# Layer 0's row passes: partial sums put into the PSUM banks by ScalarE, and a bias table built with one Sign pass

## The chip, the core and the metric

The kernel runs on one core of a Trainium2 chip. The metric is the device time in microseconds, the median of several runs. TensorE multiplies matrices into eight PSUM banks, VectorE, ScalarE and GpSimd do elementwise work, and SyncE's queue (SP) issues nearly all transfers. Each engine takes its instructions in order and meets the others through semaphores.

## What is computed

Two blocks on x of shape (1, 256, 2048), float32. The first has two layers:

```python
for l in range(DEPTH):                                   # two layers
    h = rmsnorm(x, norm_gain[l]) * (1 + scale) + shift   # scale, shift, gate = silu(c) @ w_mod[l] + b_mod[l]
    proj = h @ w_in[l]                                   # q_a, k_a, v_a, g_a, q_i, k_i, w_i, q_b, k_b, v_b, g_b
    # sparse attention: top 64 keys by the index scores, logits get a bias:
    bias = rel_bias[t5_bucket(pos_q - pos_k)]            # 32 buckets x 8 heads
    # retention on q_b, k_b, v_b
    x = x + gate * (concat([y_a, y_b]) @ w_out[l])
```

`t5_bucket` gives a distance of 0 to 15 its own bucket and puts larger ones into 16 buckets that widen logarithmically. The second block (convolution, a gated linear recurrence, two output projections, a gated embedding) is not touched.

## The kernel before

Float32 products are made of three matmuls each: an operand is split into a high and a low part (`hi`, `lo`), and hi x hi, hi x lo and lo x hi are summed. `wchunk` does this for weights: one transfer of two k-tiles by up to 512 columns into `raw` (512 KB, three buffers, L231), a cast on ScalarE that gives `whi` (L236), and a subtraction on VectorE that gives `wlo` (L238). `wgroup` runs over the chunks of a column group and, for each chunk, over the two row tiles t = 0, 1, with six matmuls for each (L254 to L256, in the order hi x hi, hi x lo, lo x hi); both row tiles have a bank of their own out of four (`mmt`), so two groups fit at once. When a group is done its consumer empties the two banks.

In `layer`, ten column groups of 512 (one of 336) columns are not computed at once. In layer 0 the normalized rows hT become ready in four quarters of four k-tiles, since each quarter needs a vector-matrix product with w_mod (`gemv`, 16 transfers of 512 KB and 16 VectorE multiply-adds at L357 per quarter). So the ten groups are swept four times (q = 0 to 3), two chunks a group. The consumer in these passes is `spill`: in pass q = 0 ScalarE copies each bank to a tile `held` (L931; the tiles are named sp and gate), in passes 1 to 3 VectorE adds the bank to it (L934), and pass 3 hands the sum on. Layer 1 has two passes.

From pass q = 1 on a background generator builds the bias table, advanced by 0.75 steps for each chunk (`step`, `RATE["t5"]`). `rel_rotary` writes the clipped distances as bytes to DRAM (`reld`, L422). `bias_table` reads them back spread over 128 partitions (`load`, L461, tile `rb`): partition p compares with bucket p % 32. Three ScalarE passes over 512 columns (Abs L483, Relu L484, Relu L486) make a one-hot matrix, two matmuls (L469) with the high and low part of the bias values look the biases up, ScalarE copies the result out (L471), and it is stored to DRAM (`biasd`, L472). There are 12 loads of 1024 bytes per partition; one is issued half a job ahead. `until("select")` in pass q = 3 emits what is left of it.

The order on each engine is made by a list scheduler from the order of emission and from priorities: `tc.high_priority(offset=n)` moves an instruction n places forward (`AHEAD`: 20 for a weight's transfer, 30 for its cast, 35 for its subtraction). On the chip each queue keeps the order that the scheduler gave it.

## Time and profile before

| | |
|---|---|
| median of 3 runs | 1931.42 us (1928.2 to 1932.54) |
| the profiled execution | 1935.11 us, span 1933.3 us |
| TensorE busy (matmuls) | 1841.2 us, 95% |
| VectorE busy | 1310.0 us, 68% |
| ScalarE busy | 1041.2 us, 54% |
| moved by DMA | 440.37 MB, mean 228 GB/s |

The span runs from the first to the last instruction of one execution. Busy time of TensorE is that of its matmuls, whose shown ends overlap the next matmul's start. A wait is told as the one who waited, the one who ended the wait, and the idle time before it.

### The profile page before, as it was taken

The page shows a single profiled execution, that of the slowest core. Times are in us where ns is not written, and L with a number is a line of the kernel's source. Part 1 is how long each engine was busy: PE and PEld are TensorE (multiplying, and loading weights), DVE is VectorE, ACT ScalarE, POOL GpSimd, SP SyncE. Part 2 cuts the span into 40 slices and gives each one's busy share as a digit, 9 for nine tenths or more (in the row PEclk, how much of TensorE's full clock was granted, in tenths as well). Part 3 has the DMA queues.
Part 4 walks back from the last instruction along what each step waited for, and adds up shares of the span by engine and source line. Part 5 has one row for each costly group of instructions (what it writes and reads, how often), then busy time and mean ns, then how long its engine had stood idle before and what let it go on. Part 6 is the DMA issues. An engine that isn't in the chain of part 4 may idle for free.

```text
span 1933.3 us, 24130 instructions
## 1 busy us (share of the span) xinstructions
PE 1841.2 (95%) x8670; PEld 1500.1 (78%) x8670; DVE 1310.0 (68%) x1705; ACT 1041.2 (54%) x1576; POOL 109.0 (6%) x220
## 2 busy tenths in 40 slices
PE   3989999998989999999999999999999999999997
PEld 3867677777867787788778778878887888888886
DVE  6788889988667779966655656656665545555564
ACT  3567674645445546356455764466545444445554
POOL 2000040002010005000110000000000000000100
PEclk9999999999989999999999999999999999999998
DMA  9988888887888999865557665556556666656664
GB/s 315 319 289 290 274 296 259 289 290 237 295 281 269 314 301 312 274 202 157 161 184 219 205 186 163 155 161 197 164 151 191 194 191 193 195 185 218 186 202 146
DMA packets 230921, 440.37 MB, mean 228 GB/s; under 512 B 19728, under 2 KB 32144, under 8 KB 230672
## 3 DMA queue, kind: packets, MB, share of 16 engines
q1 hardware_dynamic: 228880, 436.38, 71.3%
q10 hardware_dynamic: 1440, 2.34, 0.4%
q8 instruction: 68, 1.11, 0.2%
q14 instruction: 53, 0.43, 0.1%
q0 software_dynamic: 480, 0.10, 0.0%
HBM read 430.85 MB, written 7.91 MB: 227 GB/s over the span
## 4 chain that ended last, share of the span: by engine, by line
PE 64%; DMA 14%; DVE 10%; ACT 5%; issue 5%; POOL 2%; SPq 1%; ACTq 0%; DVEq 0%; POOLq 0%
PE mm L255 19%; PE mm L256 19%; PE mm L254 19%; DMA graw<-in_w_mod_dram 6%; DVE wlo L238 4%; DVE acc L357 2%; DMA rb<-reld 2%; DMA raw<-in_w_in_dram 2%; ACT whi L236 2%; PE tr L201 2%; DMA raw<-in_w_out_dram 1%; PE tr L1153 1%; DMA dec<-in_k_dec_dram 1%; DMA L<-biasd 1%; DMA raw<-in_w_mod_dram 1%
## 5 line engine op out<-in xcount | busy, mean ns | idle before, releaser
L238 DVE TENSOR_TENSOR wlo<-raw,whi 128x1024 fp32r<-128x1024 f32 (+1 forms) x596 | 721.0, 1212 | 408.8 <-ACT whi L236 407.0
L236 ACT CAST whi<-raw 128x1024 fp32r<-128x1024 f32 (+1 forms) x596 | 620.9, 1044 | 676.0 <-PE mm L256 437.2
L255 PE MATMUL mm<-wlo,ah 128*128 128x512 f32 (+1 forms) x2368 | 933.6, 394 | 14.1 <-DVE wlo L238 13.8
L254 PE MATMUL mm<-whi,ah 128*128 128x512 f32 (+1 forms) x2368 | 933.8, 397 | 13.7 <-ACT ah L192 7.8
L256 PE MATMUL mm<-whi,al 128*128 128x512 f32 (+1 forms) x2368 | 931.0, 393 | 0.5 <-DVE al L193 0.3
L255 PEld LDWEIGHTS mm<-wlo,ah 128*128 128x128 f32 x2368 | 447.5, 189 | 119.8 <-DVE wlo L238 32.6
L254 PEld LDWEIGHTS mm<-whi,ah 128*128 128x128 f32 x2368 | 446.4, 189 | 109.7 <-ACT whi L236 10.4
L256 PEld LDWEIGHTS mm<-whi,al 128*128 128x128 f32 x2368 | 447.1, 189 | 93.0 <-DVE al L193 2.4
L357 DVE SCALAR_TENSOR_TENSOR acc<-graw,ct,acc 128x1024 f32<-128x1024 f32 x174 | 222.7, 1280 | 51.5 <-DMA graw<-in_w_mod_dram 50.9
L934 DVE TENSOR_TENSOR sp<-sp,mm 128x512 f32<-128x512 f32 (+1 forms) x64 | 41.8, 657 | 8.4 <-PE mm L256 8.2
L201 PE MATMUL tr<-blob,ev 128*128 128x128 f32 x192 | 35.8, 277 | 11.5 <-DVE ev L1181 3.8
L184 ACT ACTIVATE ev<-tr,vT 128x128 f32<-128x128 f32 x112 | 32.4, 375 | 17.1 <-PE tr L201 17.1
L201 PEld LDWEIGHTS tr<-blob,ev 128*128 128x128 f32 x192 | 24.1, 141 | 21.2 <-issue 8.4
L156 POOL TENSOR_SCALAR rv<-tot 128x1 f32<-128x1 f32 (+1 forms) x9 | 2.8, 307 | 660.2 <-DVE tot L208 646.8
L504 ACT ACTIVATE junk<-xs 128x512 bf16<-128x512 f32 (+1 forms) x42 | 25.6, 610 | 22.1 <-DMA xs<-in_x_dram 10.0
L158 POOL TENSOR_TENSOR ry<-rv,mhalf 128x4 f32<-128x4 f32 (+2 forms) x33 | 31.8, 965 | 2.7
L201 PE MATMUL tr<-blob,xs 128*128 128x128 f32 x128 | 24.2, 281 | 5.3 <-ACT xs L995 3.6
L1153 PEld LDWEIGHTS tr<-X 128*128 128x128 f32 x224 | 27.0, 192 | 2.0 <-ACT uT L1203 1.0
L483 ACT ACTIVATE oh<-rb,blob 128x512 f32<-128x512 uint8 x24 | 16.4, 717 | 22.5 <-DMA rb<-reld 22.5
L1153 PE MATMUL tr<-X 128*128 128x128 f32 x224 | 27.5, 276 | 0.1
L156 POOL TENSOR_SCALAR rv<-ssq 128x4 f32<-128x4 f32 x12 | 4.5, 371 | 402.4 <-ACT junk L504 402.2
L156 POOL TENSOR_SCALAR rv<-var 128x4 f32<-128x4 f32 x8 | 5.2, 645 | 361.5 <-DVE var L853 361.3
(275 smaller groups left out, 1227.3 us busy)
## 6 DMA issues: line engine op xcount, KB each, us to landing
raw<-in_w_in_dram SPq DMA_DIRECT2D x416, 512.0 KB
graw<-in_w_mod_dram SPq DMA_DIRECT2D x186, 512.0 KB
raw<-in_w_out_dram SPq DMA_DIRECT2D x64, 512.0 KB
raw<-in_w_o_dram SPq DMA_DIRECT2D x32, 512.0 KB
raw<-in_w_ple_gate_dram SPq DMA_DIRECT2D x32, 512.0 KB
raw<-in_w_a_out_dram SPq DMA_DIRECT2D x16, 512.0 KB
raw<-in_w_b_out_dram SPq DMA_DIRECT2D x16, 512.0 KB
raw<-in_w_in_dram SPq DMA_DIRECT2D x16, 256.0 KB
```

Of the source, the lines that this page charges most:

```text
L158: G.tensor_tensor(y, v, mhalf[:, 0:n], op=OP.pow)
L184: A.activation(e[:, s], ps[:, s], AF.Copy, scale=gain[:, i:i + 1])
L201: T.transpose(ps[:, s], src[:, s], ident)
L236: A.copy(hi, raw)
L238: V.tensor_sub(lo, raw, hi.bitcast(F32))
L254: T.matmul(o, ah, hi[:, j, :], start=first, stop=False)
L255: T.matmul(o, ah, lo[:, j, :], start=False, stop=False)
L256: T.matmul(o, al, hi[:, j, :], start=False, stop=end)
L357: last[0] = V.scalar_tensor_tensor(acc, rf, ct[:, j:j + 1], acc, op0=OP.mult, op1=OP.add)
L504: A.activation(junk[:, :n], src, AF.Square, accum_out=acc)
L934: V.tensor_add(h, h, pt[:, :n])
L1153: T.matmul(ps[:, h * P:(h + 1) * P], X[:, h, s], X[:, h, s], start=True, stop=True)
```

## The change

In passes 1 and 2 of layer 0 VectorE no longer adds the bank to `held`. Instead ScalarE copies `held` into the bank before the group's first matmul, which then accumulates on it (`start` is false), and copies the bank out again at the group's end, as in pass 0. The copies in get a priority offset of 10. Pass 3 and layer 1 stay.

The one-hot matrix becomes a matrix of signs of (distance + 0.5 - lower edge), one ScalarE pass of 512 columns; the bias values are replaced by half differences between neighbouring buckets (`rsh` holds the values shifted by one bucket), so that the signed sum gives the same bias. There are 6 loads of 2048 bytes per partition, two are issued at the start, and the load for job n + 2 is issued with the last pass of job n, into the buffer which that pass reads. Six empty steps stand between the first loads and the first pass.

```diff
+            if sums:
+                with tc.high_priority(offset=AHEAD["sums"]):      # 10
+                    for t in (0, 1):
+                        A.copy(pts[t][:, :n], sums[t][:, :n])
@@ mms
-                    first = ci == 0 and j == 0
+                    first = ci == 0 and j == 0 and not sums
@@ bias_table
+            rsh = ap.tile([P, 32], F32, name="rsh", tag="dec", bufs=2)
+            V.memset(rsh, 0.0)
             for g in range(4):
-                G.dma_start(rbd[32 * g:32 * g + 32, 8 * g:8 * g + 8], a["rel_bias"])
+                c = slice(8 * g, 8 * g + 8)
+                G.dma_start(rbd[32 * g:32 * g + 32, c], a["rel_bias"])
+                G.dma_start(rsh[32 * g + 1:32 * g + 32, c], a["rel_bias"][0:31])
+                G.dma_start(rsh[32 * g:32 * g + 1, c], a["rel_bias"][31:32])
+            V.scalar_tensor_tensor(rbd, rsh, turn, rbd, op0=OP.mult, op1=OP.add)
+            V.tensor_scalar(rbd, rbd, 0.5, None, op0=OP.mult)
@@
-            jobs = [(0, r) for r in range(0, 32, 8)] + [(1, r) for r in range(0, 32, 4)]
+            jobs = [(0, 0), (0, 16)] + [(1, r) for r in range(0, 32, 8)]
@@ load
-                rb = ap.tile([P, 1024 // ns, ns], U8, name="rb", tag="rb", bufs=2)
+                rb = ap.tile([P, 2048 // ns, ns], U8, name="rb", tag="sc", bufs=2)
@@
-            nxt = load(*jobs[0])
+            rbs = [load(*job) for job in jobs[:2]]
+            for _ in range(6):
+                yield
             for n, (t, r0) in enumerate(jobs):
-                for hf in range(2):
-                    oh = ap.tile([P, 512], F32, name="oh", tag="sc", bufs=2)
-                    A.activation(oh, rb[:, hf * h2:(hf + 1) * h2, :].rearrange("p a b -> p (a b)"), AF.Abs, bias=bmid)
-                    A.activation(oh, oh, AF.Relu, bias=bhw)
+                for i in range(4):
                     ohr = ap.tile([P, 512], F32R, name="ohr", tag="qT", bufs=8)
-                    A.activation(ohr, oh, AF.Relu, bias=ones[:, 0:1], scale=-1.0)
-                    if hf == 0 and n + 1 < len(jobs):
-                        nxt = load(*jobs[n + 1])
+                    A.activation(ohr, rbs[n][:, i * h2:(i + 1) * h2, :].rearrange("p a b -> p (a b)"), AF.Sign, bias=edge)
+                    if i == 3 and n + 2 < len(jobs):
+                        rbs.append(load(*jobs[n + 2]))
                     yield
@@ layer, spill
-                        if q == 0:
-                            if gi not in (3, 4):
+                        if q < per - 1:
+                            if q:
+                                pass
+                            elif gi not in (3, 4):
                                 held[gi, t] = wp.tile([P, 512], F32, name="sp", tag="al" if t else "ah", bufs=16)
@@
-                            if q == per - 1:
-                                return cons(t, held[gi, t], True)
-                    wgroup(srcs, n, hT, rows, spill, "first" if l and not q and not gi else "k")
+                            return cons(t, held[gi, t], True)
+                    wgroup(srcs, n, hT, rows, spill, "first" if l and not q and not gi else "k",
+                           sums=[held[gi, t] for t in (0, 1)] if 0 < q < per - 1 else None)
```

## Rows read from the trace of the kernel before

**Rows 1.** The page: busy us (share of the span) and instructions.
```profile
PE 1841.2 (95%) x8670; PEld 1500.1 (78%) x8670; DVE 1310.0 (68%) x1705; ACT 1041.2 (54%) x1576; POOL 109.0 (6%) x220
```
**Rows 2.** Stretches: length; PE, PEld, DVE, ACT, POOL busy (count); clock, DMA share, GB/s.
```profile
60.00:100.00 40.00, 40.00 (x187) 33.15 (x186) 30.84 (x30) 24.05 (x35) 0.00 (x0) 1.00 0.97 331
100.00:240.00 140.00, 129.38 (x570) 97.32 (x569) 116.39 (x145) 99.11 (x153) 2.61 (x2) 1.00 0.87 284
```
**Rows 3.** Waits, 100 to 240 us: us in total, times, longest us.
```profile
ACT oh L483 <- DMA rb<-reld: 22.5, 8, 4.6
...
ACT whi L236 <- DMA raw<-in_w_in_dram: 8.4, 8, 3.2
...
PE mm L254 <- ACT whi L236: 5.7, 5, 1.4
PE mm L255 <- DVE wlo L238: 4.6, 6, 1.8
```
**Rows 4.** TensorE's timeline: start, length, instruction, idle time before, what ended it.
```profile
111.95 0.50 PE L255 MATMUL mm<-wlo,ah 128*128 128x512 f32 x1 [1.79 <-DVE wlo L238]
...
123.26 0.73 PE L254 MATMUL mm<-whi,ah 128*128 128x512 f32 x2 [1.21 <-ACT whi L236]
...
215.45 0.73 PE L254 MATMUL mm<-whi,ah 128*128 128x512 f32 x2 [1.23 <-ACT whi L236]
```
**Rows 5.** ScalarE's timeline, two of its waits for the table's loads.
```profile
120.32 1.34 ACT L483 ACTIVATE oh<-rb,blob 128x512 f32<-128x512 uint8 x2 [3.11 <-DMA rb<-reld]
...
212.51 0.72 ACT L483 ACTIVATE oh<-rb,blob 128x512 f32<-128x512 uint8 x1 [3.56 <-DMA rb<-reld]
```
**Rows 6.** ScalarE's groups, 100 to 240 us: count, busy us, mean ns, idle before.
```profile
L486 ACT ACTIVATE ohr<-oh,blob 128x512 fp32r<-128x512 f32 x20 | 14.4, 718 | 0.0
L484 ACT ACTIVATE oh<-oh,blob 128x512 f32<-128x512 f32 x20 | 14.2, 711 | 0.0
L483 ACT ACTIVATE oh<-rb,blob 128x512 f32<-128x512 uint8 x20 | 13.6, 716 | 22.5 <-DMA rb<-reld 22.5
L471 ACT COPY bt<-ms 32x512 f32<-32x512 f32 x19 | 10.7, 564 | 1.1 <-DMA biasd<-bt 1.0
...
L931 ACT COPY sp<-mm 128x512 f32<-128x512 f32 x2 | 1.2, 576 | 0.0
```
**Rows 7.** VectorE's additions, 100 to 240 us, same columns.
```profile
L934 DVE TENSOR_TENSOR sp<-sp,mm 128x512 f32<-128x512 f32 x28 | 19.0, 683 | 7.9 <-PE mm L256 7.7
L934 DVE TENSOR_TENSOR gate<-gate,mm 128x512 f32<-128x512 f32 x8 | 5.3, 681 | 0.5 <-PE mm L256 0.5
...
L934 DVE TENSOR_TENSOR sp<-sp,mm 128x336 f32<-128x336 f32 x4 | 2.0, 503 | 0.5 <-PE mm L256 0.5
```
**Rows 8.** ScalarE's copies out of the banks, 60 to 100 us, same columns.
```profile
L931 ACT COPY sp<-mm 128x512 f32<-128x512 f32 x8 | 4.7, 587 | 8.5 <-PE mm L256 8.5
...
L931 ACT COPY sp<-mm 128x336 f32<-128x336 f32 x2 | 0.9, 442 | 1.2 <-PE mm L256 1.2
```
**Rows 9.** ScalarE's timeline in pass q = 0, at a group's end.
```profile
76.32 0.59 ACT L931 COPY sp<-mm 128x512 f32<-128x512 f32 x1 [2.27 <-PE mm L256]
77.68 0.59 ACT L931 COPY sp<-mm 128x512 f32<-128x512 f32 x1 [0.77 <-PE mm L256]
78.16 1.05 ACT L236 CAST whi<-raw 128x1024 fp32r<-128x1024 f32 x1
```
**Rows 10.** Waits of SP's queue, 100 to 240 us, columns as rows 3.
```profile
SPq L231 <- DVE wlo L238: 49.5, 27, 3.7
...
SPq L422 <- DVE tmp L421: 6.5, 2, 5.4
```
**Rows 11.** ScalarE's timeline: the first two table loads.
```profile
2.70 1.28 ACT L290 ACT_TABLE_LOAD   x1 [2.70 <-issue]
...
338.98 1.28 ACT L720 ACT_TABLE_LOAD   x1
```
**Rows 12.** GpSimd's timeline: the loads of the bias values.
```profile
37.92 2.13 POOL L447 DMA_DIRECT2D rbd<-in_rel_bias_dram  x4 [11.39 <-DVE vT L319]
```

More of the change, by code (lines that the diff above doesn't have):

```diff
@@ L31 @@
         "hgrn": 0.66}
-AHEAD = {"wdma": 20, "whi": 30, "wlo": 35, "gdma": 0, "gdve": -10, "tail": -5}
+AHEAD = {"wdma": 20, "whi": 30, "wlo": 35, "gdma": 0, "gdve": -10, "tail": -5, "sums": 10}
 WJ, NB = 12, 6
@@ L48, in shape_constants @@
     lo = np.array([edge[b] for b in i % 32], f)
-    hi = np.array([edge[b + 1] - 1 for b in i % 32], f)
-    lo, hi = -(lo + hi) / 2, (lo - hi) / 2
+    lo, hi = f(0.5) - lo, np.where(i % 32 == 0, f(1), f(-1))
     ones = np.ones((P, P), f)
@@ L239, in wchunk, with wgroup @@
             return hi, lo
-        def wgroup(srcs, n, aT, kts, consumer, mode="k", tw=3):
+        def wgroup(srcs, n, aT, kts, consumer, mode="k", tw=3, sums=None):
             pts = [mmt(), mmt()]
+            if sums:
+                with tc.high_priority(offset=AHEAD["sums"]):
+                    for t in (0, 1):
+                        A.copy(pts[t][:, :n], sums[t][:, :n])
             chunks = [kts[i:i + 2] for i in range(0, len(kts), 2)]
@@ L250, in mms @@
                     ah, al = ah[:, kt % 4, :], al[:, kt % 4, :]
-                    first = ci == 0 and j == 0
+                    first = ci == 0 and j == 0 and not sums
                     end = ci == last and j == 1
                     o = pts[t][:, :n]
-                    T.matmul(o, ah, hi[:, j, :], start=first, stop=False)
-                    T.matmul(o, ah, lo[:, j, :], start=False, stop=False)
-                    T.matmul(o, al, hi[:, j, :], start=False, stop=end)
+                    skip = sums is not None
+                    T.matmul(o, ah, hi[:, j, :], start=first, stop=False, skip_group_check=skip)
+                    T.matmul(o, ah, lo[:, j, :], start=False, stop=False, skip_group_check=skip)
+                    T.matmul(o, al, hi[:, j, :], start=False, stop=end, skip_group_check=skip)
             held = range(0)
@@ L288, in build @@
         ident, tri, inv = blob[:, 0:128], blob[:, 128:256], blob[:, 256:320]
-        bmid, bhw, ones = blob[:, 320:321], blob[:, 321:322], blob[:, 322:450]
+        edge, turn, ones = blob[:, 320:321], blob[:, 321:322], blob[:, 322:450]
         A.activation(ct, ct, AF.Silu)
@@ L494, in bias_table @@
                         store.append(look_up(*held.pop(0)))
-                yield
+                    if i % 2:
+                        yield
             store.pop()()
```

8 lines of the change are left out of this document (3 added, 5 removed).

## The prediction, made before the changed kernel was run

> **What bounds the kernel now.** I read the page first. TensorE shows busy 95% of the span [rows 1], so what any edit to another engine can give back is the rest, and I have to find which part of it lies where the edit works. The change touches layer 0's row passes: four sweeps over the same ten column groups (q = 0 to 3), each with four k-tiles. The edited code runs in q = 1 and q = 2. All 40 additions of those two passes (2 x 10 groups x 2 row tiles) lie between 100 and 240 us [rows 7], and pass q = 0 runs just ahead of them.
>
> So the second view is the sums by stretch [rows 2]. The 40 us in the middle of pass q = 0 hold 187 matmuls with TensorE busy throughout and the DMA engines at 331 GB/s. The next 140 us hold 570 matmuls, 4.07 per us against 4.68. At the rate of the first stretch those 570 take 570 / 4.675 = 121.9 us: a shortage of **18.1 us**. The busy column admits 140 - 129.38 = **10.6 us** of idle time; the rest hides in matmuls whose shown ends overlap. Both are gross bounds, since a few of the matmuls counted are shorter ones. The clock is full in both stretches, so none of it is the clock.
>
> Third, the waits of that stretch [rows 3]. TensorE's own are short: 5.7 us for the cast (L254 for `whi`, ScalarE) and 4.6 us for the subtraction (L255 for `wlo`, VectorE). One step up the chain the cause shows: ScalarE stood 22.5 us in 8 waits for `rb`, the table's loads. ScalarE works in order, so a weight cast queued behind such a wait waits too. Fourth, the timelines fit this together: ScalarE's waits for `rb` [rows 5] are followed some 3 us later by a stall of TensorE for `whi` [rows 4]. That is so of four of the five stalls for `whi`; the first and the last of the four are shown, 1.21 and 1.23 us, and the longest has 1.4 us [rows 3]. Four of that size are some **5.1** of the 5.7 us.
>
> **The change part by part.** *Loads two ahead.* Now one load is in flight ahead of its use, and it lands late 8 times of 12 [rows 3]. After, each load is issued a whole job (four sign passes, six steps) before its first use, and six empty steps stand ahead of the first. At 0.75 steps per chunk six steps are eight chunks, 96 matmuls, 96 / 4.07 = 23.6 us at the pace of [rows 2], against waits of at most 4.6 us now [rows 3]. I let all waits for `rb` go: **5.1 us** of TensorE idle at least. What is late next is the ordinary raw weight (8.4 us of ScalarE waiting [rows 3]). The new load also has a wait of its own: it reuses the buffer that the job's last sign pass reads, and it stands in SP's in-order queue, ahead of weight loads. SP already waits 49.5 us in this stretch for VectorE to free raw buffers [rows 10], which covers it; uncovered it costs one sign pass, 0.72 us, for each of four loads, 2.9 us. I take 0.
>
> *One sign pass in place of three.* Of each 512 columns the Relu lines L484 and L486 go; L483 stays as Sign, with the same shape and so, I take, the same 0.72 us [rows 6]. In the stretch this frees 14.4 + 14.2 = 28.6 us of ScalarE. The six empty steps also push about four of the twenty passes and their evacuations out of the stretch: 4 x (0.716 + 0.564) = 5.1 us.
>
> Whether Sign shares the table loaded at 2.70 us, which serves all until the exponentials at 338.98 [rows 11], no row shows; bounds 0 and one load, 1.28 us of ScalarE.
> The Trainium skill ("ScalarE: Activation LUTs", section "Table sets: the hidden batching unit") names relu, copy, identity and abs as being in every set and does not name sign there; with one switch of its 2.7 us reaching TensorE in full, an estimate, the sum below would be 4.6 instead of 7.3 us, still inside the forecast's own range. No row of this kernel bears on sign.
> The other new pieces are small: one clear, one multiply-add and one halving on VectorE, each like a row of at most 0.2 us, and 8 more loads on GpSimd's queue at 2.13 / 4 = 0.53 us each [rows 12]. They run early, near 38 us [rows 12]. Eight more take 4.3 us, so VectorE may stand that long for them, with the weights' subtractions queued behind. I take 0, because nothing needs the result for a long time and the scheduler is free to put VectorE's three pieces later; 4.3 us stays as a bound.
>
> *Sums through the banks.* The 40 additions of q = 1 and 2 leave VectorE: 19.0 + 5.3 + 2.0 = 26.3 us [rows 7], from 116.4 to 90.1 us of work [rows 2]. That takes a wait for TensorE (7.7 us there) and half a microsecond ahead of many `wlo`. Of TensorE's 4.6 us for `wlo` [rows 3], 1.79 at 111.95 [rows 4] follows SP's wait of 6.5 us for the relative positions [rows 10], which stays; of the other 2.8 I count **2.0** (bounds 0 and 2.8).
> In their place ScalarE gets 40 copies out and 40 copies in. The copies out have their row: 0.587 us for 512 columns, 0.442 for 336 [rows 8]. A copy from memory into a bank is in no row; the nearest is the copy out, same shape and engine, so 0.587 is taken; with the ends 0.44 (the short copy) and 0.72 (the pass of L483) the 40 copies in would cost 6 us less or 5 us more of ScalarE. 72 x 0.587 + 8 x 0.442 = 45.8 us, less the 1.2 us of two copies already there [rows 6].
>
> The Trainium skill ("ScalarE: Activation LUTs", section "Step-by-step: what each stage is for") holds a ScalarE write to a bank to be faster than one to SBUF; that would put the copy in below the row, and the bill below at its light end.
>
> *ScalarE's bill.* 99.1 [rows 2] - 28.6 - 5.1 + 44.6 = **110.0 us**, and 22.5 us of waiting gone. Busy or held by `rb` it was 121.6. Against TensorE's 121.9 us for the stretch it is 90% full: near, but not the bound. VectorE's 90.1 us falls far below. The transfers, 284 x 140 us = 39.8 MB, take 120 us at the 331 GB/s that pass q = 0 shows, so nothing below 120 us is to be had.
>
> *What the full queue costs.* A copy out waits on ScalarE for the last matmul of its group, and the next casts stand behind it. Pass q = 0 lives with that: ScalarE waits for TensorE 8.5 us ahead of eight copies [rows 8], TensorE stays full. But the row at 77.68 shows the cast straight behind the second copy out, no gap between [rows 9]. A copy in that lands in the 0.77 us gap before 77.68 is free; one that lands between copy out and cast delays the cast, and the next chunk, by 0.587. Bounds: 0, and 20 groups x 0.587 = 11.7 us. The scheduler sets a cast 30 places ahead and a copy in 10, and the copy has a whole group (some 5.5 us) before its matmul needs it, so I take a fifth of the groups: **2.3 us** lost.
>
> *The hidden shortage.* 18.1 - 10.6 = 7.5 us are short delays that no wait row names. With loads on time and VectorE a quarter lighter I count a third, **2.5** (bounds 0 and 7.5).
>
> Sum: 5.1 + 2.0 + 2.5 - 2.3 = 7.3 us saved. The passes after q = 2 follow TensorE, so I pass it on in full. Against the profiled execution's 1935.1 us that is 1927.8; this execution lies 3.7 us above the median of the runs, so for the median: 1931.4 - 7.3 = **1924.1 us**. With the hidden shortage at 0 and at 7.5, and the rest as taken, its own range is 1919 to 1927.
>
> **The rivals.** *All stalls go.* With the `rb` waits gone and VectorE light the stretch runs as pass q = 0 does, but for what hangs on SP's wait at its start (1.8 us and as much hidden): 18.1 - 3.6 = 14.5 us, **1916.9**. For it: q = 0 ran full with copies out on ScalarE. Against: q = 0 had no table and no copies in, and the DMA engines would have to give 39.8 MB in 125.5 us, 317 GB/s.
>
> *ScalarE becomes the bound and gives the gain back.* One copy in stands ahead of the cast in nearly every group: the 11.7 us bound in place of 2.3, 9.6 - 11.7 = 2.1 us lost, **1933.5**, no change that can be measured. For it: 90% full with waits in order; against: the six empty steps and the halved table.
>
> *Slower: both copies in land between copy out and cast.* The price is 20 x 2 x 0.587 = 23.5 us less the 9.6 gained: 13.9 us, **1945.3**. The place is ScalarE's queue at each group's end; it decides as soon as ScalarE no longer gets its gaps before a copy out (2.27 and 0.77 us in [rows 9]), when its work per group passes TensorE's: 110.0 / 20 = 5.5 us against 121.9 / 20 = 6.1. So copies and waits a tenth dearer than taken would do it.
>
> **How the numbers follow.** About 0.2% (3.9 us) is what a measurement of this kernel can tell from no change. Forecast 0.50, all stalls gone 0.17, gain given back 0.20, slower 0.13. Faster: 0.47 of the forecast, 0.17, and 0.01 of the third = 0.65; same: 0.03 + 0.18 = 0.21; slower: 0.01 + 0.13 = 0.14. The range leaves out the slower rival and thin ends: from 1913.5 (the whole 18.1 us) to 1935 (the gain given back, with some of the smaller bounds on top).
>
> **What would show it.** Right: no wait of ScalarE for `rb`; in 100 to 240 us over 4.4 matmuls per us; ScalarE near 110 us of work and VectorE near 90 in what were those 140 us; pass q = 3's first addition some 7 us earlier, and that distance kept to the end. Wrong: TensorE waiting for the new copies at L254, or for `whi` behind them; a table load between 2.7 and 338 us; VectorE standing near 48 us for the small loads of the bias values; SP waiting for a sign pass; or the distance lost again later in the kernel.

## The result, and the profile after

The changed kernel takes **1944.59 us** (median, 1939.92 to 1947.37) against 1932.54 us (1928.2 to 1937.44) for the kernel before, measured beside it: a ratio of 1.0057, interval 1.004 to 1.0074. It is slower by about 12 us. The forecast was 1924.1 us, in a range of 1913.5 to 1935.0: wrong in sign and outside the range. The profiled execution took 1947.37 us, its span is 1945.6 us.

The page of the kernel after: busy us (share of the span) and instructions, beside [rows 1].

```profile
PE 1845.9 (95%) x8670; PEld 1505.6 (77%) x8670; DVE 1289.7 (66%) x1668; ACT 1050.8 (54%) x1608; POOL 116.6 (6%) x228
```

The work moved as the diff says: VectorE has 20.3 us less, ScalarE 9.6 us more, TensorE the same 8670 matmuls. The sums by stretch, columns as in [rows 2]:

```profile
60.00:100.00 40.00, 40.00 (x186) 33.04 (x185) 31.65 (x31) 24.74 (x35) 0.00 (x0) 1.00 0.98 347
100.00:240.00 140.00, 125.01 (x533) 92.92 (x532) 89.15 (x101) 102.04 (x174) 2.43 (x2) 0.98 0.83 268
```

Pass 0 is as before. In the next 140 us TensorE gets through 533 matmuls where it did 570, 3.81 per us against 4.07, and is busy 125.01 us where it was 129.38. The prediction asked for over 4.4 per us. The DMA engines move less too, 268 GB/s against 284. The waits of the same stretch, beside [rows 3]:

```profile
DVE wlo L237 <- ACT whi L235: 42.9, 28, 5.0
ACT sp L946 <- PE mm L262: 20.5, 13, 2.7
...
PE mm L260 <- ACT whi L235: 7.0, 5, 3.3
ACT whi L235 <- DMA raw<-in_w_in_dram: 6.9, 5, 3.4
PE mm L261 <- DVE wlo L237: 6.5, 12, 0.8
ACT ohr L498 <- DMA rb<-reld: 4.1, 2, 2.7
...
ACT gate L946 <- PE mm L262: 2.8, 3, 1.2
```

The waits for the table's loads fell, as meant: 4.1 us in 2 against 22.5 in 8. In their place ScalarE now stands 20.5 + 2.8 = 23.3 us in the copies out (L946), waiting for the last matmul of a group. VectorE stands 42.9 us for casts, against 12.4 us in the same view of before:

```profile
DVE wlo L238 <- ACT whi L236: 12.4, 15, 1.5
```

TensorE's own waits grew from 5.7 + 4.6 to 7.0 + 6.5 us. ScalarE's groups of the stretch (count, busy us, mean ns, idle before) and then some moments of its timeline:

```profile
L946 ACT COPY sp<-mm 128x512 f32<-128x512 f32 x28 | 16.1, 583 | 19.6 <-PE mm L262 19.6
L248 ACT COPY mm<-sp 128x512 f32<-128x512 f32 x27 | 15.4, 591 | 0.2
L498 ACT ACTIVATE ohr<-rb,blob 128x512 fp32r<-128x512 uint8 x16 | 10.8, 714 | 4.1 <-DMA rb<-reld 4.1
...
L248 ACT COPY mm<-gate 128x512 f32<-128x512 f32 x8 | 4.5, 594 | 0.0
```
```profile
108.40 0.59 ACT L946 COPY sp<-mm 128x512 f32<-128x512 f32 x1 [1.60 <-PE mm L262]
108.89 1.05 ACT L235 CAST whi<-raw 128x1024 fp32r<-128x1024 f32 x1
...
120.55 0.72 ACT L498 ACTIVATE ohr<-rb,blob 128x512 fp32r<-128x512 uint8 x1 [1.42 <-DMA rb<-reld]
...
129.20 1.04 ACT L235 CAST whi<-raw 128x1024 fp32r<-128x1024 f32 x1 [3.35 <-DMA raw<-in_w_in_dram]
...
150.25 0.59 ACT L946 COPY sp<-mm 128x512 f32<-128x512 f32 x1 [1.85 <-PE mm L262]
151.40 0.59 ACT L946 COPY sp<-mm 128x512 f32<-128x512 f32 x1 [0.57 <-PE mm L262]
151.88 1.11 ACT L248 COPY mm<-sp 128x512 f32<-128x512 f32 x2
152.92 2.00 ACT L235 CAST whi<-raw 128x1024 fp32r<-128x1024 f32 x2
```

The trace also records when a weight has landed: each of these transfers signals sixteen times, and the last signal counts. The weight that is cast at 108.89 had landed at 107.72, the one that is cast at 152.92 at 149.90. Ahead of the first cast ScalarE stood 1.60 us for TensorE, ahead of the second 1.85 and 0.57 us, and there both copies in came before the cast too. Over the 38 casts of 100 to 240 us landed weights stood 62.1 us until they were cast, over the 42 of the kernel before 27.6 us. Of the 62.1 us some 27.3 went to copies out (13.1 of it their wait for TensorE) and 12.1 to copies in. At 129.20 there is another cause, a cast that waited 3.35 us for its raw weight. TensorE's longest stall in the two passes is the consequence (start, length, instruction, idle before):

```profile
130.30 0.75 PE L260 MATMUL mm<-whi,ah 128*128 128x512 f32 x2 [3.29 <-ACT whi L235]
```

**Where the 12 us are.** Taking the n-th weight matmul of both traces and subtracting the start times: the kernel after is 0.6 us ahead at the start of pass 1, 4.3 behind in the middle of pass 1, 2.1 at its end, 7.2 at the end of pass 2, 9.9 at the end of pass 3 (near 317 us). So 7.8 us are lost in the two edited passes and 2.7 in the one behind them. Then the distance falls, to 2.2 us at 745 us, and grows again to 12.2 at the end. It grows in four short places: from 2.2 to 8.2 near 752 us, from 5.2 to 8.9 near 995, and by 1.6 each near 1274 and 1476. In all four the granted clock of the kernel after is at 1.2 GHz, the lower of its two levels, for 3.4 or 6.8 us; in the kernel before it is at 2.4 GHz throughout the same work. One of these places, after and then before (start and length, busy by engine, clock, DMA share, GB/s):

```profile
990.00:1005.00 15.00, 12.20 (x42) 8.96 (x41) 5.53 (x7) 3.88 (x9) 0.00 (x0) 0.77 0.45 140
```
```profile
985.00:1000.00 15.00, 13.24 (x61) 9.66 (x61) 9.41 (x12) 6.96 (x15) 0.00 (x0) 1.00 0.55 177
```

The mean clock of an execution is 0.984 to 0.986 after and 0.986 to 0.992 before, so by the means (0.9885 - 0.9852) x 1940 = 6.4 us of the 12 would lie in the clock, an estimate. Why it falls in these later places, which the change doesn't touch, is open.

### The profile page after: what moved, and what is told of

Its sections match the earlier page's. It is cut to its first block, busy times and chain, and to the rows that moved or that the text cites. A ratio compares the mean times of both kernels' runs of the same rounds, so it can differ in the third digit from the quotient of the medians.

```text
span 1945.6 us, 24133 instructions
## 1 busy us (share of the span) xinstructions
PE 1845.9 (95%) x8670; PEld 1505.6 (77%) x8670; DVE 1289.7 (66%) x1668; ACT 1050.8 (54%) x1608; POOL 116.6 (6%) x228
## 4 chain that ended last, share of the span: by engine, by line
PE 68%; DMA 11%; DVE 9%; ACT 5%; issue 4%; POOL 2%; SPq 0%; ACTq 0%; DVEq 0%; POOLq 0%
PE mm L261 21%; PE mm L262 21%; PE mm L260 20%; DVE wlo L237 4%; DMA raw<-in_w_in_dram 3%; DMA graw<-in_w_mod_dram 3%; ACT whi L235 2%; DMA raw<-in_w_out_dram 2%; PE tr L200 2%; DVE acc L363 2%; PE tr L1168 1%; DMA L<-biasd 1%; POOL ry L157 1%; PE tr L371 1%; DMA ev<-in_b_mod_dram 1%
## 5 line engine op out<-in xcount | busy, mean ns | idle before, releaser
L261 PE MATMUL mm<-wlo,ah 128*128 128x512 f32 (+1 forms) x2368 | 934.9, 395 | 17.2 <-DVE wlo L237 17.0
L946 ACT COPY sp<-mm 128x512 f32<-128x512 f32 (+1 forms) x64 | 35.5, 565 | 30.1 <-PE mm L262 29.9
L200 PE MATMUL tr<-blob,ev 128*128 128x128 f32 x192 | 36.2, 280 | 11.3 <-DVE ev L1196 3.8
L183 ACT ACTIVATE ev<-tr,vT 128x128 f32<-128x128 f32 x112 | 32.4, 375 | 17.2 <-PE tr L200 17.2
L200 PEld LDWEIGHTS tr<-blob,ev 128*128 128x128 f32 x192 | 24.2, 142 | 20.5 <-issue 8.5
L200 PEld LDWEIGHTS tr<-blob,xs 128*128 128x128 f32 x128 | 16.6, 146 | 12.9 <-ACT xs L1010 6.9
```

Of the source, the lines that this page charges most:

```text
L183: A.activation(e[:, s], ps[:, s], AF.Copy, scale=gain[:, i:i + 1])
L200: T.transpose(ps[:, s], src[:, s], ident)
L261: T.matmul(o, ah, lo[:, j, :], start=False, stop=False, skip_group_check=skip)
L946: A.copy(held[gi, t][:, :n], pt[:, :n])
```

## The experiments

Three theories stood at the start, by the letters that the expectations use. **A, order**: the copies out wait on ScalarE's in-order queue for TensorE and hold the next casts. **B, work**: ScalarE simply has too much to do. **C, the table's new form** (longer loads, the buffer it shares, six empty steps). The later expectations add **D**: the table's transfers, on SP's in-order queue, hold the raw weights behind them; and its rival **E**: the transfers' own landing time, or ScalarE's wait for the first `rb`, sets the passes.

Besides the time I use one measure from each trace: how long TensorE takes from the 241st to the 721st weight matmul, which is passes 1 and 2 whatever the shift. "Delay" is what the starts in it lie further apart than the median for their shape, at full clock; what falls into half-clock stretches stands behind a plus. Each of these comes from one profiled execution, which for some kernels lies far from the median time: 9.5 us above it in e4, 5.2 above in e3, 2.8 above in the changed kernel, 6.2 below in e18, 5.0 below in e16, 3.9 below in e13. ACT and DVE are busy us in 100 to 240 us.

| kernel | median us | ratio to before | passes 1-2, us | delay, us | ACT | DVE |
|---|---|---|---|---|---|---|
| before | 1931 to 1935 | 1 | 134.8 | 16.8 | 99.1 | 116.4 |
| changed | 1944.59 | 1.004 to 1.0074 | 142.6 | 23.5 + 3.0 | 102.0 | 89.2 |
| e1 table alone | 1933.99 | 0.9977 to 1.0009 | 135.3 | 17.2 + 1.5 | 70.8 | 116.4 |
| e2 sums alone | 1944.3 | 1.0024 to 1.0062 | 145.3 | 26.1 + 1.7 | 126.4 | 89.3 |
| e3 out on VectorE | 1932.15 | 0.9976 to 1.0008 | 135.3 | 17.2 + 1.5 | 92.3 | 116.1 |
| e4 in on VectorE | 1939.88 | 1.0019 to 1.0052 | 140.4 | 18.5 + 5.8 | 87.4 | 112.0 |
| e5 out behind casts | 1939.58 | 1.0015 to 1.0039 | 135.3 | 17.1 + 1.7 | 107.6 | 94.8 |
| e7 table in pass 3 | 1958.96 | 1.012 | 121.6 | 9.4 + 3.2 | 98.7 | 98.1 |
| e8 table alone, 4 raw | 1927.92 | 0.9955 to 0.9981 | 136.9 | 18.9 + 1.5 | 70.5 | 115.3 |
| e10 table, no adds | 1937.39 | 0.9991 to 1.0027 | 136.6 | 17.0 + 3.1 | 71.5 | 93.8 |
| e11 table on GpSimd's queue | 1947.1 | 1.0034 to 1.0072 | 135.4 | 11.9 + 6.9 | 71.9 | 115.4 |
| e13 e5 + that + 4 raw | 1932.58 | 0.9971 to 1.0 | 126.4 | 11.0 | 111.5 | 102.8 |
| e15 e5 + 4 raw | 1933.51 | 0.9983 to 1.0012 | 139.0 | 16.4 + 6.1 | 105.2 | 92.4 |
| e16 changed + 4 raw | 1933.85 | 0.999 to 1.0015 | 141.0 | 20.2 + 4.8 | 103.4 | 90.2 |
| e17 e5 + 4 raw + loads on GpSimd's | 1928.03 | 0.9949 to 0.9981 | 127.7 | 9.8 + 1.4 | 111.5 | 99.3 |
| e18 e5 + loads on GpSimd's | 1938.74 | 1.0004 to 1.0042 | 133.9 | 15.9 + 1.5 | 108.9 | 95.8 |
| e19 table alone, loads on GpSimd's | 1941.77 | 1.0026 to 1.006 | 141.1 | 17.8 + 6.9 | 66.3 | 110.0 |
| e20 changed, loads on GpSimd's | 1946.23 | 1.0039 to 1.0083 | 142.3 | 21.5 + 4.4 | 102.8 | 89.4 |

### Each half alone

The table alone puts the spill back:

```diff
-                        if q < per - 1:
+                        if q == 0:
@@
-                            return cons(t, held[gi, t], True)
+                            if q == per - 1:
+                                return cons(t, held[gi, t], True)
@@
-                           sums=[held[gi, t] for t in (0, 1)] if 0 < q < per - 1 else None)
+                           sums=None)
```

> The sign pass and the loads two ahead alone; passes 1 and 2 add on VectorE as in the kernel before. Theory A (order: the copies out wait on ScalarE for the group's last matmul and hold the casts behind them): the table is innocent, 3 to 8 us faster than before, 1925 to 1929 us, no wait of ScalarE for rb. Theory B (work: ScalarE simply has too much to do in the two passes): 28 us of ScalarE work less, also 1925 to 1929. Theory C (the table's new form is the cause: long loads, steps that come later): as slow as the changed kernel, 1940 to 1946.

The sums alone take the old `bias_table` back:

```diff
-                    A.activation(ohr, rbs[n][:, i * h2:(i + 1) * h2, :].rearrange("p a b -> p (a b)"), AF.Sign, bias=edge)
+                    A.activation(oh, rb[:, hf * h2:(hf + 1) * h2, :].rearrange("p a b -> p (a b)"), AF.Abs, bias=bmid)
+                    A.activation(oh, oh, AF.Relu, bias=bhw)
+                    A.activation(ohr, oh, AF.Relu, bias=ones[:, 0:1], scale=-1.0)
```

> The sums through the banks alone, with the old table (three passes, one load ahead). A: at least as slow as the changed kernel, 1944 to 1952, ScalarE waiting some 20 us for TensorE at its copies out. B: clearly slower than the changed kernel, 28 us more ScalarE work in the stretch, 1955 to 1965. C: as fast as before or faster, 1925 to 1932.

Waits of 100 to 240 us, e1 first, then e2:

```profile
ACT whi L235 <- DMA raw<-in_w_in_dram: 36.3, 21, 3.8
...
ACT ohr L498 <- DMA rb<-reld: 10.1, 4, 3.3
```
```profile
DVE wlo L238 <- ACT whi L236: 39.1, 34, 4.1
...
ACT sp L940 <- PE mm L263: 3.2, 2, 1.6
```

The loss comes with the sums: e2 is as slow as the whole change, and e1 takes the time of before. So C by itself is no cause of the loss. But e1 also shows the missing gain: it was expected at 1925 to 1929 us by A and B alike and took 1933.99. ScalarE has 28 us less to do (70.8 against 99.1), and passes 1 and 2 take 135.3 against 134.8 us: its waits for `rb` halved (22.5 to 10.1 us) and its waits for raw weights went from 8.4 to 36.3 us. The freed time became waiting for the next input. Of the 21 late weights of e1's row 20 took 3.2 to 7.8 us from issue to landing, hardly more than the 3.5 to 7.1 us of those cast in 60 to 100 us: they were issued late. In e2 ScalarE is busy 126.4 of 140 us and hardly waits for TensorE at all (3.2 us), where A had expected some 20 us. So full a queue would explain the loss by B, without the order; that is argued, as no run has e2's work in another order, and its time (1944.3 us) lies below B's own 1955 to 1965.

### The same sums, in another place or order

```diff
 e3
-                            A.copy(held[gi, t][:, :n], pt[:, :n])
+                            (V.tensor_copy if q else A.copy)(held[gi, t][:, :n], pt[:, :n])
 e4
-                        A.copy(pts[t][:, :n], sums[t][:, :n])
+                        V.tensor_copy(pts[t][:, :n], sums[t][:, :n])
 e5
-                A.copy(hi, raw)
+                cast[0] = A.copy(hi, raw)
@@ spill
+                    def later(dst, src):
+                        yield
+                        yield
+                        with tc.issue_after(cast[0].ins):
+                            A.copy(dst, src)
+
+                        if 0 < q < per - 1:
+                            return later(held[gi, t][:, :n], pt[:, :n])
```

> As the changed kernel, but in passes 1 and 2 VectorE copies the banks out; ScalarE keeps the copies in. A: ScalarE has no wait for TensorE in the stretch, VectorE waits less than 10 us for casts beyond the 12 of before, and the loss is gone: 1922 to 1931. B: half of the added work is gone, half of the loss: 1936 to 1940. C: no effect, 1940 to 1946.

> As the changed kernel, but VectorE copies the sums into the banks; ScalarE keeps the copies out. A: the wait for TensorE stays on ScalarE, and so does the loss: 1940 to 1946. B: half of the loss, 1936 to 1940. C: no effect, 1940 to 1946.

> As the changed kernel, same work on every engine, but each copy out of passes 1 and 2 stands on ScalarE behind both casts of the next group. Theory A (order: casts held behind copies that wait for TensorE): ScalarE waits for TensorE at its copies less than 8 us in 100 to 240 us (23 in the changed kernel), VectorE waits for casts under 20 us (45), and the time falls to that of before or below, 1918 to 1932. Theory B (work): still 1940 to 1946, since nothing is taken off ScalarE.

Waits of 100 to 240 us in e3, in e4, then in e5, then e5's stretch:

```profile
ACT mm L248 <- DVE sp L946: 18.6, 17, 2.1
```
```profile
ACT sp L946 <- PE mm L262: 28.7, 19, 4.9
```
```profile
DVE wlo L239 <- ACT whi L237: 36.1, 31, 4.6
ACT whi L237 <- DMA raw<-in_w_in_dram: 20.0, 15, 3.3
```
```profile
100.00:240.00 140.00, 128.77 (x566) 98.54 (x565) 94.79 (x106) 107.59 (x184) 2.54 (x2) 0.99 0.87 280
```

These three test A against B. e5 takes no work from ScalarE; each copy out is only issued behind a later cast. ScalarE's waits for TensorE leave the list, 566 matmuls fit in place of 533, and passes 1 and 2 take 135.3 instead of 142.6 us, though ScalarE is busier (107.6 us). e3 removes the copies out from ScalarE and arrives at the same 135.3. There ScalarE's copies in now stand 18.6 us for VectorE's copies out, and the passes lose nothing by it: a wait in the queue costs only where a landed weight stands behind it. Those stood 62.1 us in the changed kernel, 52.7 in e4, 37.2 in e5 and 31.8 in e3. e4 takes the copies *in* away, nearly as much work: ScalarE is down to 87.4 us, yet its waits for TensorE rise to 28.7 us and the passes take 140.4 us. With the new table, then, it is the order that costs, A, some 7 us of the passes. How much the copies in cost beside it is less sharp: in e4 more of the delay falls into half-clock stretches (18.5 + 5.8 us against 23.5 + 3.0), and e4's profiled execution is a long one.

The totals say less than the passes. e3 takes the time of before; e5 ends as high as e4, 5 us above before and 5 us below the changed kernel, between what A (1918 to 1932) and B (1940 to 1946) had led to expect. By matched matmuls e5 is 0.3 us *ahead* of before at the end of pass 2 and 5.5 behind at the end of pass 3: what the new order gains is lost in the pass behind it. That the last of the moved copies meet the additions of pass 3 there is a guess; no run isolates it. And none of the three gets below before.

### Without the table, without the additions

In e7 the table starts in pass 3:

```diff
-                if l == 0 and q == 1:
+                if l == 0 and q == 3:
```

> As the changed kernel, but the table is started with pass 3 instead of pass 1, so passes 1 and 2 have only the sums on ScalarE, some 80 us of work in 140. Theory A: passes 1 and 2 are still slow, ScalarE waiting 25 us or more for TensorE at its copies out, and the stretch from 100 to 240 us holds no more than 545 matmuls. Theory B: passes 1 and 2 run full, over 580 matmuls in that stretch (the changed kernel 533, before 570). The whole time is not the point here, as the table is crowded into pass 3; 1935 to 1955.

```profile
100.00:240.00 140.00, 132.37 (x591) 106.51 (x590) 98.09 (x107) 98.71 (x158) 1.29 (x2) 0.98 0.87 292
```
```profile
ACT sp L946 <- PE mm L262: 14.3, 13, 1.8
```

591 matmuls and a delay of 9.4 + 3.2 us, with ScalarE 98.7 us busy and still waiting 14.3 us for TensorE in `sp` alone. Against the kernel before, about 9 us of the shorter time are matmuls of others, the lookups above all, which are not in these passes. By the marks set beforehand this is B's case (over 580 matmuls) and not A's (545 at most). Landed weights stand 72.4 us there, so that is no loss by itself either: a weight takes 4.7 us to land, against 5.5 in the changed kernel, and TensorE does not run short. The sums on ScalarE are thus bearable as long as no table runs beside them: it takes both. The total suffers because pass 3 then holds the table (28 us of delay there).

In e10 the table stands alone and the additions of passes 1 and 2 are left out:

```diff
-                            V.tensor_add(h, h, pt[:, :n])
-                            return cons(t, held[gi, t], True)
+                            if q == per - 1:
+                                V.tensor_add(h, h, pt[:, :n])
+                                return cons(t, held[gi, t], True)
```

> The table alone, and the 40 additions of passes 1 and 2 left out (the sums of these passes are lost); nothing takes their place. It gives the ceiling of what relieving VectorE can bring. If VectorE bounds the stretch: 26 us of its work less, over 600 matmuls in 100 to 240 us, 1917 to 1924. If the transfers or their issue do: under 580 matmuls there, 1928 to 1936.

```profile
ACT whi L235 <- DMA raw<-in_w_in_dram: 34.8, 22, 4.5
DVE wlo L237 <- ACT whi L235: 32.3, 27, 5.4
```

This is the ideal of both halves of the change: VectorE freed of the additions (93.8 us busy) and ScalarE not charged for them (71.5). The passes take 136.6 us, no less than before; 3.1 us of the delay lie in half-clock stretches, and what is left, 17.0 us, is that of before. So the gains that the prediction counted for `rb`, for `wlo` and for a lighter VectorE were not to be had with three raw buffers and the table's loads on SP. ScalarE waits for raw weights, and VectorE for ScalarE.

### What holds the raw weights

Why is a raw weight late when SP's queue has nothing else to wait for than the buffer? Two candidates: the three buffers are too few, or other transfers stand in front on SP (D). e8 is e1 with a fourth raw buffer, and one `ev` buffer less to make room; e11 moves the table's three transfers to GpSimd's queue.

```diff
 e8
-RAW, GRAW, WB, EV = 3, 3, 3, 5
+RAW, GRAW, WB, EV = 4, 3, 3, 4
 e11
-                Y.dma_start(reld[t], rb[:, 0:(t + 1) * P])
+                G.dma_start(reld[t], rb[:, 0:(t + 1) * P])
@@ load
-                Y.dma_start(rb, bass.AP(tensor=reld[t].tensor, offset=reld[t].offset + r0 * ns,
+                G.dma_start(rb, bass.AP(tensor=reld[t].tensor, offset=reld[t].offset + r0 * ns,
@@ store
-                return lambda: Y.dma_start(bass.AP(tensor=biasd[t].tensor, offset=biasd[t].offset + r0 * ns,
+                return lambda: G.dma_start(bass.AP(tensor=biasd[t].tensor, offset=biasd[t].offset + r0 * ns,
```

> The table alone (VectorE adds in passes 1 and 2), with four buffers for raw weights instead of three and four instead of five evacuation tiles. ScalarE waited 36 us for raw weights in the stretch with the table alone. If the ring of three buffers is what delays them: under 15 us of such waits, 600 matmuls or more in the stretch, 1920 to 1928. If VectorE's work is: as the table alone, 1929 to 1938.

> The table alone (VectorE adds in passes 1 and 2), with all of the table's transfers (the distances' store, the loads of rb, the stores of the result) issued from GpSimd's queue instead of SP's, which carries the weights. Theory D (the stalls of passes 1 and 2 come from raw weights queued on SP behind the table's waits): ScalarE waits for raw weights under 20 us in 100 to 240 us (36 with the table alone), over 590 matmuls in that stretch, 1922 to 1929. Theory E (the transfers' own landing time, or the wait of ScalarE for the first rb, sets them): no change beyond 3 us, 1930 to 1937.

e8 is 6 us faster than before, but not here: passes 1 and 2 take 136.9 us. By matched matmuls it is 0.8 us ahead of before at the end of pass 3, 8 by 745 us and 10 by 1050 us. More buffers alone pay later in the kernel. e11's waits in 100 to 240 us:

```profile
ACT whi L235 <- DMA raw<-in_w_in_dram: 39.6, 19, 5.2
...
ACT ohr L498 <- DMA rb<-reld: 14.1, 3, 8.5
...
POOL biasd L487 <- ACT bt L486: 88.3, 13, 17.8
```

By its own marks e11 speaks against D: 39.6 us of waits for raw weights where D asked for under 20, and 562 matmuls where it asked for over 590. Only pass 2 gains, its delay falls to 3.6 us (6.5 in e1). In pass 1 the table's own data comes later (8.5 us of waiting at once), and the stores, which wait for ScalarE, keep GpSimd 88.3 us from its own arithmetic, which pass 3 needs (delay 14.3 us there). The total is 13 us above e1's; as an improvement it failed. Two runs that belong to it were no better. e12, the same with four raw buffers, took 1948.87 us (passes 1 and 2 in 135.2), outside what either theory gave. e14, without the additions, took 1946.08 us (135.9), within 2 us of e11 as E had it.

> The same with four raw buffers and four evacuation tiles (the table alone with four raw buffers gave 1927.9). D: the gains add, 1916 to 1923. E: as with four raw buffers, 1925 to 1931.

> The table alone with its transfers on GpSimd's queue, and the 40 additions of passes 1 and 2 left out (their sums are lost). With the transfers on SP leaving out the additions gave nothing (560 matmuls in 100 to 240 us against 566). D: now it gives something, over 600 matmuls and 4 us or more against the same kernel with the additions. E: nothing again, within 2 us.

### Putting the causes together

e13 has e5's order, e11's queue and e8's buffers. e15 and e16 are e5 and the changed kernel with four raw buffers (the one line of e8). e17 to e20 leave the stores of the table (L487) on SP and move only its `reld` store and its loads to GpSimd (the first two hunks of e11): e17 with e5's order and four buffers, e18 with e5's order and three, e19 with the table alone, e20 with nothing else.

> The changed kernel with the copies out behind the next group's casts, the table's transfers on GpSimd's queue and four raw buffers. If, once weights are no longer late, VectorE's 26 us of additions hold the passes: 2 us or more faster than the same without the sums, 1912 to 1921. If ScalarE's copies still hold the casts: slower than the same without the sums, 1925 to 1934.

> The changed kernel with the copies out behind the next group's casts and four raw buffers, all transfers on SP. With the table on GpSimd's queue too, passes 1 and 2 took 126 us (before 135). If the fourth buffer did that: passes 1 and 2 under 130 us, over 590 matmuls in 100 to 240 us, the whole 1920 to 1928. If GpSimd's queue did it: 133 us or more, under 575 matmuls, 1930 to 1937.

> The changed kernel with four raw buffers, nothing else. If the order on ScalarE (copies out ahead of casts) is what costs, a fourth buffer ahead of the casts cannot mend it: 5 us or more above the same with the copies behind the casts, 1930 to 1942. If the casts only come late because raw weights do: within 2 us of it.

> As the first of these three, with the distances' store and the loads of rb on GpSimd's queue, but the stores of the table's result left on SP, so that GpSimd's norm arithmetic in pass 3 does not stand behind them. If that is what cost pass 3 its 9 us: passes 1 and 2 under 130 us and pass 3's stalls under 5 us, 1917 to 1925. If not: 1927 to 1935.

> The changed kernel, copies out behind the next group's casts, the distances' store and the loads of rb on GpSimd's queue; three raw buffers as before. With four raw buffers this took 127.7 us for passes 1 and 2 and 1928.0 in all. If SP's queue alone withheld the gain: passes 1 and 2 at 126 to 130 us, 1925 to 1932. If it needs the fourth buffer: 133 us or more, 1932 to 1940.

> The table alone (VectorE adds), with the distances' store and the loads of rb on GpSimd's queue, three raw buffers. If VectorE's additions hold the passes once the weights come on time: 3 us or more longer in passes 1 and 2 than the same with the sums. If not: within 2 us of it, and the sums bring nothing.

> The changed kernel with its order on ScalarE as it is, and the distances' store and the loads of rb on GpSimd's queue. If the order costs by itself: passes 1 and 2 at 134 us or more, 5 us above the same with the copies behind the casts. If it cost only because the weights were late: within 2 us of it.

The stretch 100 to 240 us, e17 first, then e15 (loads on SP), e18 (three buffers) and e20 (three buffers, order of the change):

```profile
100.00:240.00 140.00, 135.27 (x604) 105.39 (x602) 99.32 (x112) 111.47 (x191) 6.83 (x10) 0.99 0.92 296
```
```profile
100.00:240.00 140.00, 126.95 (x549) 98.58 (x549) 92.38 (x105) 105.21 (x181) 3.23 (x2) 0.95 0.86 272
```
```profile
100.00:240.00 140.00, 129.00 (x571) 100.34 (x570) 95.77 (x108) 108.85 (x186) 7.12 (x10) 0.99 0.92 289
```
```profile
100.00:240.00 140.00, 126.20 (x535) 95.27 (x535) 89.38 (x101) 102.76 (x174) 6.83 (x10) 0.96 0.87 270
```

With both loosened, e17, the passes take 127.7 us, 7.1 less than before; with the loads left on SP 139.0, with three buffers 133.9. ScalarE is busier than in any other kernel with the new table but e13 (111.5 us in both), and TensorE gets through more matmuls than in the rest, 604 and 605. So B isn't what limits these two. ScalarE's waits for raw weights are 5.6 us in e17; then the same row of e18, and of e15, where one alone lasts 5.7 us:

```profile
ACT whi L237 <- DMA raw<-in_w_in_dram: 5.6, 6, 2.2
```
```profile
ACT whi L237 <- DMA raw<-in_w_in_dram: 19.9, 14, 3.4
```
```profile
ACT whi L237 <- DMA raw<-in_w_in_dram: 16.9, 7, 5.7
```

SP's timeline in e15 shows what D means, and ScalarE's what came of it. The store of the distances waits 6.0 us for VectorE, and the weights' transfers come out in a row once it has gone; then the table's loads take their turn among them:

```profile
108.44 0.34 SPq L430 DMA_DIRECT2D reld<-tmp  x1
108.83 2.49 SPq L232 DMA_DIRECT2D raw<-in_w_in_dram  x5
111.42 0.69 SPq L478 DMA_DIRECT2D rb<-reld  x1
...
112.87 0.63 SPq L478 DMA_DIRECT2D rb<-reld  x1
114.48 1.34 SPq L232 DMA_DIRECT2D raw<-in_w_in_dram  x1
```
```profile
129.22 1.04 ACT L237 CAST whi<-raw 128x1024 fp32r<-128x1024 f32 x1 [5.68 <-DMA raw<-in_w_in_dram]
```

But the weight of that longest wait did not stand in the queue for long: it is the one issued at 114.48, behind the two loads, and it was on its way for 14.7 us. Twelve of its sixteen landing signals had come by 122.1 us, the other four at 128.2 to 129.2. In the changed kernel the weight cast at 129.20 was issued at 116.80, had twelve signals by 123.2 and the last at 129.18; the table's two loads, issued at 112.14 and 115.86, landed 8.4 and 11.6 us later. In 100 to 240 us the last signal of a weight comes at most 6.0 us behind its twelfth in the changed kernel and 7.1 in e15, but 4.1 in the kernel before and 3.0 and 2.7 in e17 and e18. So the table's larger loads on SP delay four of the sixteen parts of the weights issued behind them. How much of D is this and how much waiting in the queue, no run separates: moving the loads changes both.

e18 and e20 differ in the order of the copies out alone: 133.9 against 142.3 us, 1938.74 against 1946.23 us. That is theory A a second time, with another queue (in the passes from a short execution of the one and a long one of the other, so the medians, 7.5 us apart, are the safer measure).

With three buffers the queue alone does little: e18 against e5 133.9 and 135.3 us, e20 against the changed kernel 142.3 and 142.6, and e19 against e1 is even longer, 141.1 and 135.3, with 6.9 us of its delay at half clock. e19 took 7.2 us longer in the passes than e18, which by its expectation says that the additions on VectorE hold the passes; at full clock the delays are only 1.9 us apart (17.8 and 15.9), so this stays open. D is thus shown together with the fourth buffer and e5's order (e17 and e13 against e15), and not by itself. e17 and e13 differ in the table's stores alone (SP or GpSimd): the passes are equal to 1.3 us, the totals differ by 4.5, which is what a store waiting on GpSimd costs pass 3 (delay 8.7 us in e13, 4.9 in e17).

Misses: e16 was expected some 5 us above e15, and the totals are equal (1933.85 and 1933.51); with four buffers on SP the order does not show in the time of the kernel, and hardly in the passes (141.0 and 139.0). e13 and e17 gained in the passes and missed the totals that should have come of it, 1912 to 1921 and 1917 to 1925 us. e18 came out as expected if the fourth buffer is needed (133 us or more, 1932 to 1940). Of e15's 11.3 us above e17 some 6.1 lie in half-clock stretches, the first behind its longest stall (6.15 us between two starts at 124 us), so the split between order, buffers and queue is good to a few microseconds only.

**A version that beats both.** e17 takes 0.9965 (0.9949 to 0.9981) of the time of before. But e8, with the old additions, is as fast (1927.92 against 1928.03 us). That the sums on ScalarE pay in the total is therefore not shown; shown is that the gain in passes 1 and 2 exists once the queue and the buffers let it. The table alone with four buffers, its loads on GpSimd's queue *and* its stores on SP wasn't tried.

## Why the prediction was wrong, point by point

**What bounds the kernel** was read one link short. The shortage of 18.1 us in passes 1 and 2 is there, and ScalarE's 22.5 us of waiting for `rb` too [rows 3]. But the step "One step up the chain the cause shows" made a cause of what was only the last wait to show. Taking it away (e1) or nearly every other load on VectorE and ScalarE (e10) left the passes at 135.3 and 136.6 us against 134.8. Behind it stood the raw weight, whose buffer comes free late and whose transfer queues on SP. [rows 10] showed both, 49.5 us of SP waiting for a buffer and 6.5 us for the distances, and I read the 49.5 as *cover* for a new wait. It was the limit. An estimate from the rows of before: a weight takes 6.3 us from issue to landing (the median of 100 to 240 us), its cast 1.05 and its subtraction 1.22, so one of three buffers comes round every 8.6 / 3 = 2.9 us, while TensorE needs 12 matmuls x 0.227 = 2.7 us for what it holds. In 60 to 100 us, where pass 0 runs full, the weights take 4.9 us to land, which makes 7.2 / 3 = 2.4 us.

**"Loads two ahead", 5.1 us**: the waits fell (22.5 to 4.1 us) and no gain followed. "What is late next is the ordinary raw weight" named the right successor and gave it no price; in e1 it rose from 8.4 to 36.3 us. The six empty steps did nothing like the 23.6 us I gave them: the first sign pass runs at 120.55 us, the moment its load has landed, the first pass of the old table at 120.32 [rows 5]. I take it that the steps delay only the emission, and that the scheduler places the instruction; no run shows it. Every kernel with the new table in these passes and its loads on SP also has a stall near 121 to 131 us, 2.3 to 6.9 us between two starts of matmuls, where the kernel before has 1.6. In the changed kernel and in e15 it is the late landing told above; with the loads on GpSimd's queue it is gone in e13 and e17 only (0.9 us), in the others 2.2 to 4.2 us remain. SP's wait for a sign pass, which I took as 0, is in no row.

**"Sums through the banks", 2.0, and the hidden shortage, 2.5**: failed for the same reason (e10). The sizes of the pieces held: 0.583 and 0.591 us for copies out and in against 0.587 taken, 0.714 for a sign pass against 0.716 in [rows 6].

**ScalarE's bill** held: 102.04 us for 533 matmuls is 109.1 for 570, against 110.0. VectorE comes to 89.15 x 570 / 533 = 95.3 against 90.1.

**"What the full queue costs", 2.3 us, is the step that turned the sign.** I priced a copy as its own 0.587 us, and worried about the copies *in*. What costs is a copy *out* that stands in the queue ahead of casts and waits for TensorE: up to 2.7 us a time, 23.3 us in all, and what of it holds a landed weight (13.1 us) is passed to the next chunk. Pass 0 "lives with that", and so does e7 in passes 1 and 2, where no table stands beside the sums; with the table it doesn't, although its work per group, 109.1 / 20 = 5.5 us, stayed below TensorE's 6.1. The same work in another order takes 135.3 instead of 142.6 us (e5), and again 133.9 instead of 142.3 (e18, e20): the term measured 7.3 us where I had 2.3, and the gains beside it 0 (e1, e10) where I had 9.6.

**The slower rival**, 1945.3 us at a chance of 0.13, met the time by luck, and the place (ScalarE's queue at a group's end) by reasoning, but only half of the mechanism. Copies in do come between out and cast, as at 151.88 us, and take 12.1 of the 62.1 us for which landed weights stand. But it was not decided by ScalarE's work passing TensorE's, and it does not carry the loss: taking the copies in off ScalarE (e4, a long execution) mends 2.2 of the 7.8 us in the passes, putting the copies out behind the casts 7.3. Of the 12 us some 7.8 are lost in the passes and 2.7 in pass 3, and the rest comes and goes later; "passed on in full" was too simple. Between 332 and 745 us the kernel regains 8 us. e1, e3 and e8, which have the new table too, gain about 4, 4 and 7 us on before in the same stretch, and e2, which has the old one, 0.7: the table seems to pay there, for all that the passes don't show. By which step, no run tells. One end of the range was off by a little: 1931.4 less the whole 18.1 us is 1913.3, not 1913.5.

**The small bounds.** GpSimd's extra loads did hold VectorE, near the place named, but with no effect: 2.80 us of a bound of 4.3, and the kernel is 0.6 us ahead 50 us later.

```profile
50.24 0.25 DVE L461 SCALAR_TENSOR_TENSOR rbd<-rsh,blob,rbd 128x32 f32<-128x32 f32 x1 [2.80 <-DMA rsh<-in_rel_bias_dram]
```

Sign needed no table load: the loads of ScalarE's tables come at 2.62 and then, for the exponentials, at 348.36 us, and none between. The Trainium skill ("ScalarE: Activation LUTs", section "Table sets: the hidden batching unit") doesn't name sign among the functions that every set has; here 24 sign passes ran beside the set in use with no load between, and the 2.7 us that the page gives for a switch did not arise.

## What to carry to other kernels

Where an engine works in order, a cheap instruction that waits for a slow partner costs its wait to whatever stands ready behind it: before moving an evacuation onto the engine that feeds TensorE, ask what stands behind it, and issue the feeding work first. A wait that is removed pays only if the input behind it is early: look at the queue that loads it and at who frees its buffers, and price the successor, or give the chain one more buffer and a queue free of the side work's transfers together with the edit. Look at when the last part of a transfer lands, and not only at when it was issued. Try the ideal of an edit (here the additions simply left out) before trusting its gain.

## What the runs showed of the hardware

A copy by ScalarE into a bank took no less than one out of it: 0.591 and 0.594 us against 0.583 for 128x512. The Trainium skill ("ScalarE: Activation LUTs", section "Step-by-step: what each stage is for") holds a write to a bank to be faster than one to SBUF. These two copies differ in their source too. With SBUF as the source of both, the rows agree with the page by a little: ScalarE's cast of 128x512 from SBUF to SBUF (L191, to fp32r) took 0.611 us.

The table's loads on SP made the weights behind them land late in part: four of sixteen signals up to 6.0 us behind the twelfth in the changed kernel, up to 7.1 in e15, and at most 3.0 and 2.7 in e17 and e18, where the loads go by GpSimd's queue.

The granted clock fell behind some long stalls of TensorE: in the changed kernel 3.4 us at 1.2 GHz follow the stall of 3.29 us that ended at 130.3 us, and 3.4 us more follow one of 1.39 us near 220 us; in e15 6.8 us begin within the longest, of some 6 us. The trace of before, whose longest stall in these passes is 1.79 us [rows 4], has none there. So a long stall can be paid for twice. But not every one was followed by a fall (e2 has one of 3.09 us between two starts at 192 us, and stays at 2.4 GHz), and e2 is as slow as the change at the clock of before (0.9887), so the loss doesn't hang on it.
